# Seven block products per pair of column tiles: another order, and banks opened by ScalarE copies

## The chip, the cores and the metric

The kernel runs on one core of one Trainium2 chip. The metric is the device time of one execution in microseconds (us). The engines in this text: PE is TensorE (matmuls), PEld its loading of weights, DVE is VectorE, ACT is ScalarE, POOL is GpSimd, SP is SyncE, which here only issues DMAs.

## The reference, cut to what matters

One encoder block over 1024 positions and 1024 channels, batch 1, float32. The part that the change touches is the one big input projection of the normed input:

```python
hn = rms_norm(h, norm_in)
z = jnp.einsum('bsd,de->bse', hn, w_in)
zq, zkv, zkr, g_attn, u_pool, g_pool, g_merge = jnp.split(z, IN_SPLITS, axis=-1)
y_attn = mla_attention(zq, zkv, zkr, q_norm, w_uq, kv_norm, w_ukv) * jax.nn.silu(g_attn)
y_pool = multiscale_pool(u_pool, pool_w, pool_scale) * jax.nn.silu(g_pool)
a = jnp.einsum('bsc,cd->bsd', y_attn, w_branch_attn)
p = jnp.einsum('bsc,cd->bsd', y_pool, w_branch_pool)
gate_a, gate_p = jnp.split(jax.nn.sigmoid(g_merge.astype(jnp.float32)).astype(h.dtype), 2, axis=-1)
merged = gate_a * a + gate_p * p
h = h + jnp.einsum('bsd,de->bse', merged, w_out)
```

`g_attn`, `u_pool`, `g_pool` and `g_merge`, 3584 columns of `z`, are 28 tiles of 128 columns.

## The kernel before, in words

Every matrix product is made of three: each operand is split into a high part (rounded to the matmul's format) and a low rest, and high x high, high x low and low x high are added up. `split` (line 384) makes the two parts: a ScalarE copy (`acopy`, line 295) for the high part and a VectorE subtraction (`tt`, line 304) for the low one.

The stages: the latent projection of q (to about 40 us), the rotary key and the kv latent (to 72 us), then fourteen pairs (72 to 351 us), the up-projections (to 410 us), attention (to 566 us), the attention branch and its merge (to 616 us), and the output projection with the last norm.

A **pair** (class `Pair`, line 885) takes two of the 28 column tiles at once and all 1024 positions. Weights and input are cut into 2 x 2 blocks (two column tiles by two halves of the channels; two halves of the channels by two halves of the positions), and the four results c11, c12, c21, c22 (128 columns by 512 positions) are made with seven block products instead of eight. `ORDER` (line 889) names the weight block and the input block of each of the seven. S1 to S4 are sums and differences of weight blocks, made for each pair by VectorE (`both`, line 909); t1 to t4 are those of the input, made once (`block_sums`, line 575). `operand` (line 903) splits a weight block into a buffer of the kinds `wh` (2 buffers), `wl` (2) and `t` (45, shared by almost everything); which kind, goes by the operand's place in the order in which they are made.

A product (`product`, line 927) is 4 x 3 matmuls of 512 columns that add into one bank of PSUM. `run` (line 945) has three banks per pair: `b` is one of two buffers `p`; `a` and `c` are each one half of a two-bank tile (`ps`), and consecutive pairs take the left and the right half in turn. The sum in a bank is carried on by products that are added to what stands in it, and it is read out in between: by `acopy` or by `tt` into a result. `times` multiplies a result by the rows' 1/rms (`r`), and `posts` finish a result tile of both halves: a sigmoid or SiLU (ScalarE, the SiLU with two POOL multiplications) or the pooling windows, then a DMA that stores it.

`preps` (line 914) lists seven steps that make the operands of the *next* pair; `tick()` takes one after each product. Some pairs carry other work beside them (`beside`): `gate_pair(8, [(2, POOL_ITEMS[2]), (4, POOL_ITEMS[3])])` (line 1092) runs the third pool item's product ahead of the pair's product 2 and the fourth's ahead of product 4. A pool item loads its tile `d` two products earlier and splits it one product earlier.

None of this is the order on the engines. `Plan` (line 85) records all operations, and `order` (line 127) sets each engine's sequence by estimated costs: at each step it takes an operation that can start soonest, and among those within 30 ns of it the one written first. Each of the four `mms` groups of a product is one operation, so two products can be interleaved. Buffers of a kind are handed out in the order written. At run time every engine, and SP with its DMAs, works through its list in order and waits by semaphores.

Of the kernel before, what the change touches and what calls it, by code (L numbers as in the profile page):

```python
# [8 lines left out]
F32 = mybir.dt.float32  # L9
F32R = mybir.dt.float32r  # L10
AF = mybir.ActivationFunctionType
ALU = mybir.AluOpType
# [60 lines left out]
def real(x):  # L73
    return x.ap() if isinstance(x, View) else x
# [135 lines left out]
def hybrid_block_kernel(  # L210
# [30 lines left out]
    def buf(tag, cols, dt, name):  # L241
        uid[0] += 1
        nm = f"{name}_{uid[0]}"
        pool = pp if tag in PSUM else tp
        b = Buf(lambda: pool.tile([P, cols], dt, tag=tag, bufs=SLOTS[tag], name=nm), tag)
        b.nm = name
        return View(b, 0, P, 0, cols)
# [9 lines left out]
    def t32(name):  # L257
        return buf("t", T, F32, name)
# [5 lines left out]
    def psum(v):  # L264
        return isinstance(v, View) and v.buf.tag is not None and v.buf.tag in PSUM
# [29 lines left out]
    def acopy(o, x):  # L295
        plan.add(
            "ACT",
            lambda: nc.scalar.copy(real(o), real(x)),  # L298
            0.8333 * x.n + (155 if psum(x) else 190),
            [x],  # L300
            [o],
        )

    def tt(o, a, b, op, eng="DVE"):
        e = nc.vector if eng == "DVE" else nc.gpsimd
        c = 1.055 * a.n + 145 if eng == "DVE" else 2.2 * a.n + 150
        port = eng == "POOL" or not (psum(a) or psum(b))
        plan.add(eng, lambda: e.tensor_tensor(real(o), real(a), real(b), op), c, [a, b], [o], port=port)  # L308
# [162 lines left out]
    lft, rgt = slice(0, 512), slice(512, T)  # L471
# [4 lines left out]
    class Item:  # L476
        def __init__(self, src, width, kt, run):
            self.src, self.width, self.run, self.kt = src, width, run, kt
            self.tag = raw_tag[0]
# [75 lines left out]

    ORDER = [0, 4, 1, 5, 2, 6, 3, 7]
    raws = {k: start_loads(k) for k in ORDER[:3]}
    xs = [None] * 8
# [29 lines left out]

    for n, k in enumerate(ORDER):
        w, x = raws[k]  # L590
# [8 lines left out]
        for a in range(0, T, step_n):  # L599
            c = slice(a, a + step_n)  # L600
# [9 lines left out]
        if n + 3 < 8:  # L610
            raws[ORDER[n + 3]] = start_loads(ORDER[n + 3])
        h, l = xs[k]
# [19 lines left out]
    state = {}  # L632
# [252 lines left out]
    class Pair(Item):  # L885

        ORDER = (("A11", "b11"), ("S2", "t2"), ("S1", "t1"), ("S3", "t3"), ("A12", "b21"), ("A22", "t4"), ("S4", "b22"))

        def __init__(self, i, posts, beside=()):
            self.i, self.posts, self.beside = i, posts, dict(beside)
# [21 lines left out]
        def preps(self):  # L914
            self.ops = {}
            S, A = ALU.subtract, ALU.add
            return [
                lambda: (self.operand("A11"), self.operand("A22")),
                lambda: (self.both("S1", "A21", "A22", A, "A22"), self.both("S3", "A11", "A21", S, "A21")),
                lambda: (self.both("S2", "S1", "A11", S, "A11"), self.operand("S2")),  # L920
                lambda: self.operand("S1"),
                lambda: self.operand("S3"),
                lambda: self.operand("A12"),
                lambda: (self.both("S4", "A12", "S2", S, "A12"), self.operand("S4")),
            ]

        def product(self, bank, which, first):
# [4 lines left out]
            if which in self.beside:  # L932
                self.beside[which].go(self)
            a, b = self.ORDER[which]
            for k, ((ah, al), (bh, bl)) in enumerate(zip(self.ops[a], B[b])):
# [9 lines left out]
        def run(self, it, tick):  # L945
            if "acc" not in state:
                state["acc"] = [buf("s", T, F32, "ps") for _ in range(2)]
            half = (lft, rgt)[self.turn % 2]
            a, c = (v[:, half] for v in state["acc"])
            o1, o2 = t32("z"), t32("z")  # L950
            c11, c12, c21, c22 = o1[:, lft], o1[:, rgt], o2[:, lft], o2[:, rgt]

            def times(o, side):
                tt(o, o, state["r"][:, side], ALU.mult)

            self.product(a, 0, True)
            acopy(c21, a)
            tick()
            b = buf("p", 512, F32, "pb")
            self.product(b, 1, True)  # L960
            tt(c12, b, c21, ALU.add)
            tick()
            self.product(c, 2, True)
            tt(c22, c, c21, ALU.add)
            tick()
            self.product(b, 3, False)
            tt(c22, b, c22, ALU.add)
            times(c22, rgt)
            tick()
            self.product(a, 4, False)  # L970
            tt(c11, a, state["r"][:, lft], ALU.mult)
            tick()
            self.product(b, 5, False)
            tt(c21, b, c21, ALU.add)
            times(c21, lft)
            self.posts[1](o2)
            tick()
            self.product(c, 6, False)
            tt(c12, c, c12, ALU.add)
            times(c12, rgt)  # L980
            self.posts[0](o1)
            tick()

    loaded, ready = [0], [0]
# [203 lines left out]
    for h in range(HEADS):  # L1188
# [5 lines left out]
        for qr in range(4):  # L1194
            prs = []
            for i in (2 * qr, 2 * qr + 1):
# [17 lines left out]
                b, o = pr_of[i]  # L1214
# [33 lines left out]
            a = buf("oa", 256, F32, "oa")  # L1248
            r, c = (0, 64) if h % 2 == 0 else (64, 0)
# [14 lines left out]
    for i in range(8):  # L1264
# [9 lines left out]
        for n, (a, b) in enumerate(spans):  # L1274
            c = slice(a, b)
# [104 lines left out]
```

## Time and profile before

| what | value |
|---|---|
| median of 3 runs | 711.28 us (710.94, 711.28, 712.9) |
| the profiled execution's own time | 712.28 us |
| its span, first to last instruction | 710.2 us |
| busy: PE, DVE, ACT, POOL | 691.1 (97%), 524.2 (74%), 319.7 (45%), 104.8 us (15%) |
| matmuls | 3428 |
| granted TensorE clock, mean | 0.999 |

The time is that of the whole execution; the span leaves out what lies ahead of the first and behind the last instruction. A busy share is of the span. TensorE's matmuls are pipelined and their ends are modelled, so one is drawn longer than the distance to the next; distances from start to start are the safer measure. "[0.78 <-DVE z L308]" behind a row says that the engine was idle 0.78 us before it and that this idle time ended with VectorE's instruction of line 308 on a tile z. Line numbers are often those of a helper: 275 is every matmul, 298 every ScalarE copy, 308 every two-operand VectorE or POOL step, 377 every DMA.

### The profile page before, as it was taken

The numbers are of one execution on the slowest core, as the hardware profiler recorded it, in microseconds if no ns is written. First come the engines' busy times: TensorE is split into PE (matmuls) and PEld (weight loads), VectorE is DVE, ScalarE is ACT, GpSimd is POOL, SyncE is SP. The second block draws the span as 40 slices with busy tenths as digits, with TensorE's granted clock in tenths as the row PEclk, the third lists the DMA queues.
The fourth block names the chain that finished last, engine by engine and source line by source line (L and its number), as shares of the span: only waits on it lengthen the run. The fifth ranks groups of instructions, "written<-read, shape, count | busy, mean of one in ns | idle before, by whom it ended". The sixth has DMA issues, their size and how long they took to land.

```text
span 710.2 us, 9562 instructions
## 1 busy us (share of the span) xinstructions
PE 691.1 (97%) x3428; PEld 581.1 (82%) x3428; DVE 524.2 (74%) x823; ACT 319.7 (45%) x587; POOL 104.8 (15%) x140
## 2 busy tenths in 40 slices
PE   8999999999999999999998999999999999999996
PEld 6878888888878878888786799989999777888885
DVE  5688898777978689789869678887887859932223
ACT  5864424331423344333346467666666525421112
POOL 0020100300002030300101044545443100000000
PEclk9999999999999999999999999999999999999999
DMA  8957433122715436233777986554322499413131
GB/s 313 375 177 260 149 119 120 68 111 99 279 59 179 177 118 235 91 132 103 284 256 293 325 187 189 142 138 109 106 75 74 160 326 409 143 60 118 60 118 60
DMA packets 39567, 120.70 MB, mean 170 GB/s; under 512 B 5088, under 2 KB 6240, under 8 KB 39520
## 3 DMA queue, kind: packets, MB, share of 16 engines
q1 hardware_dynamic: 39520, 120.09, 49.4%
q8 instruction: 27, 0.44, 0.2%
q14 instruction: 20, 0.16, 0.1%
HBM read 81.14 MB, written 37.88 MB: 168 GB/s over the span
## 4 chain that ended last, share of the span: by engine, by line
PE 83%; DMA 6%; DVE 5%; ACT 2%; issue 2%; SPq 1%; DVEq 0%; ACTq 0%
PE ps L275 28%; PE pb L275 22%; PE po L275 12%; PE sc L275 7%; PE o L275 5%; PE pf L275 5%; PE pt L282 4%; DMA wr<-w_bp 2%; DMA wr<-w_uq 1%; DMA wo<-w_o 1%; DVE lo L308 1%; SPq L377 1%; DMA x<-xT 1%; DMA wr<-w_uv 1%; DVE ra L308 1%
## 5 line engine op out<-in xcount | busy, mean ns | idle before, releaser
L275 PE MATMUL pb<-t,wp 128*128 128x512 f32 x504 | 121.6, 390 | 0.0
L275 PE MATMUL ps<-xa,wp 128*128 128x512 f32 x392 | 113.0, 390 | 0.0
L275 PEld LDWEIGHTS pb<-t,wp 128*128 128x128 f32 x504 | 94.5, 188 | 19.8 <-DVE z L308 0.2
L298 ACT CAST wp<-wr 128x512 fp32r<-128x512 f32 x98 | 58.9, 619 | 102.2 <-DVE wr L308 38.3
L275 PEld LDWEIGHTS ps<-xa,wp 128*128 128x128 f32 x392 | 73.6, 188 | 15.2
L308 DVE TENSOR_TENSOR wp<-wr,wp 128x512 fp32r<-128x512 f32 x98 | 72.6, 756 | 8.8 <-ACT wp L298 8.8
L322 POOL TENSOR_SCALAR pr<-pr,small 128x384 f32<-128x384 f32 (+4 forms) x64 | 48.3, 759 | 72.1 <-DVE small L348 56.6
L290 ACT ACTIVATE pr<-sc,small 128x384 f32<-128x384 f32 (+4 forms) x64 | 47.7, 746 | 20.6 <-DVE small L357 19.7
L308 DVE TENSOR_TENSOR pT<-pt,pT 128x512 fp32r<-128x512 f32 (+1 forms) x80 | 48.6, 633 | 8.9 <-ACT pT L298 8.3
L357 DVE TENSOR_REDUCE small<-sc 128x1 f32<-128x128 f32 (+3 forms) x64 | 47.5, 750 | 9.2 <-PE sc L275 8.7
L308 POOL TENSOR_TENSOR z<-z,sig 128x512 f32<-128x512 f32 x16 | 23.5, 1493 | 199.7 <-ACT sig L290 197.3
L275 PE MATMUL po<-woh,hi 128*128 128x512 f32 (+1 forms) x136 | 51.3, 377 | 0.0
L275 PE MATMUL po<-woh,lo 128*128 128x512 f32 (+1 forms) x136 | 51.3, 377 | 0.0
L275 PE MATMUL po<-wol,hi 128*128 128x512 f32 (+1 forms) x136 | 51.2, 377 | 0.0
L298 ACT CAST pT<-pt 128x512 fp32r<-128x512 f32 (+1 forms) x80 | 41.2, 545 | 17.2 <-PE pt L282 16.5
L275 PE MATMUL o<-pT,v 128*128 128x256 f32 (+1 forms) x320 | 47.7, 282 | 0.6 <-DVE oa L308 0.4
L275 PEld LDWEIGHTS o<-pT,v 128*128 128x128 f32 x320 | 43.7, 189 | 3.2 <-DVE oa L308 0.8
L308 DVE TENSOR_TENSOR z<-pb,z 128x512 f32<-128x512 f32 x42 | 28.9, 689 | 23.3 <-PE pb L275 18.3
L308 DVE TENSOR_TENSOR res<-po,res 128x512 f32<-128x512 f32 (+1 forms) x17 | 11.2, 660 | 46.9 <-PE po L275 46.9
L275 PE MATMUL ps<-xb,wp 128*128 128x512 f32 x112 | 43.6, 389 | 0.0
L282 PE MATMUL pt<-ident,pr 128*128 128x128 f32 x288 | 42.1, 274 | 0.0
L275 PE MATMUL ps<-t,wp 128*128 128x512 f32 x168 | 41.1, 391 | 0.8 <-DVE z L308 0.8
(192 smaller groups left out, 1382.8 us busy)
## 6 DMA issues: line engine op xcount, KB each, us to landing
wr<-w_z SPq DMA_DIRECT2D x30, 512.0 KB, 4.9
gate_d<-z SPq DMA_DIRECT2D x16, 512.0 KB, 2.6
xt<-xr SPq DMA_DIRECT2D x8, 512.0 KB, 10.3
go<-gate_d SPq DMA_DIRECT2D x16, 256.0 KB, 2.8
mp_d<-go SPq DMA_DIRECT2D x16, 256.0 KB, 2.8
gate<-gate_d SPq DMA_DIRECT2D x8, 512.0 KB, 7.3
mp<-mp_d SPq DMA_DIRECT2D x8, 512.0 KB, 8.2
wo<-w_o SPq DMA_DIRECT2D x8, 512.0 KB, 8.7
```

What stands on the lines that cost most here:

```text
L275: nc.tensor.matmul(real(o), real(a), real(b), start=s, stop=e, **kw)
L282: nc.tensor.transpose(real(o), real(a), real(ident))
L290: nc.scalar.activation(real(o), real(x), func, scale=real(scale), **kw)
L298: lambda: nc.scalar.copy(real(o), real(x)),
L308: plan.add(eng, lambda: e.tensor_tensor(real(o), real(a), real(b), op), c, [a, b], [o], port=port)
L322: e.tensor_scalar(real(o), real(a), real(s1), real(s2), op0, op1)
L357: lambda: nc.vector.tensor_reduce(real(o), real(a), axis=AX.X, op=ALU.max, negate=True),
L377: lambda: nc.sync.dma_start(real(o), real(x)),
```

## The change

The seven products stay the same; their order, the bank of each, the order in which operands are made, and how results are read out are new. The first product (A11 x b11) now opens bank b, in which the running sums go on: b takes products 0, 2, 4 and 6, a takes 1, c takes 3 and 5. Results c11, c12 and c22 begin as ScalarE copies of a bank (three copies a pair, before it was one), and VectorE has seven steps on results (three additions, one multiplication out of a bank, three `times`), before it was nine.

```diff
--- before.py
+++ after.py
@@ -886,7 +886,7 @@
 
 
 
-        ORDER = (("A11", "b11"), ("S2", "t2"), ("S1", "t1"), ("S3", "t3"), ("A12", "b21"), ("A22", "t4"), ("S4", "b22"))
+        ORDER = (("A11", "b11"), ("A12", "b21"), ("S2", "t2"), ("S1", "t1"), ("S3", "t3"), ("S4", "b22"), ("A22", "t4"))
 
         def __init__(self, i, posts, beside=()):
             self.i, self.posts, self.beside = i, posts, dict(beside)
@@ -916,12 +916,12 @@
             S, A = ALU.subtract, ALU.add
             return [
                 lambda: (self.operand("A11"), self.operand("A22")),
-                lambda: (self.both("S1", "A21", "A22", A, "A22"), self.both("S3", "A11", "A21", S, "A21")),
-                lambda: (self.both("S2", "S1", "A11", S, "A11"), self.operand("S2")),
+                lambda: (self.operand("A12"), self.both("S1", "A21", "A22", A, "A22")),
+                lambda: (self.both("S3", "A11", "A21", S, "A21"), self.both("S2", "S1", "A11", S, "A11")),
+                lambda: self.operand("S2"),
                 lambda: self.operand("S1"),
-                lambda: self.operand("S3"),
-                lambda: self.operand("A12"),
-                lambda: (self.both("S4", "A12", "S2", S, "A12"), self.operand("S4")),
+                lambda: (self.operand("S3"), self.both("S4", "A12", "S2", S, "A12")),
+                lambda: self.operand("S4"),
             ]
 
         def product(self, bank, which, first):
@@ -953,32 +953,32 @@
             def times(o, side):
                 tt(o, o, state["r"][:, side], ALU.mult)
 
-            self.product(a, 0, True)
-            acopy(c21, a)
+            b = buf("p", 512, F32, "pb")
+            self.product(b, 0, True)
+            acopy(c11, b)
             tick()
-            b = buf("p", 512, F32, "pb")
-            self.product(b, 1, True)
-            tt(c12, b, c21, ALU.add)
+            self.product(a, 1, True)
+            tt(c11, a, c11, ALU.add)
+            times(c11, lft)
             tick()
-            self.product(c, 2, True)
-            tt(c22, c, c21, ALU.add)
+            self.product(b, 2, False)
+            acopy(c12, b)
             tick()
-            self.product(b, 3, False)
+            self.product(c, 3, True)
+            acopy(c22, c)
+            tick()
+            self.product(b, 4, False)
             tt(c22, b, c22, ALU.add)
             times(c22, rgt)
             tick()
-            self.product(a, 4, False)
-            tt(c11, a, state["r"][:, lft], ALU.mult)
-            tick()
-            self.product(b, 5, False)
-            tt(c21, b, c21, ALU.add)
-            times(c21, lft)
-            self.posts[1](o2)
-            tick()
-            self.product(c, 6, False)
+            self.product(c, 5, False)
             tt(c12, c, c12, ALU.add)
             times(c12, rgt)
             self.posts[0](o1)
+            tick()
+            self.product(b, 6, False)
+            tt(c21, b, state["r"][:, lft], ALU.mult)
+            self.posts[1](o2)
             tick()
 
     loaded, ready = [0], [0]
```

What becomes of it on the engines, from the two programs. On TensorE the number of instructions is the same. One place is where a pair ends and the next begins, the first pair with pool items beside it being the one that ends (the tile `ps_134` holds bank c of both pairs, one half each; `ps_133` holds bank a; `wp` are weight operands; xa and xb are parts of the input). Before:

```order
L275 MATMUL ps_134_746<-xa_53_263,wp_198_1491 128x512
L275 MATMUL ps_134_746<-xb_54_272,wp_198_1491 128x512
L275 MATMUL ps_134_746<-xa_53_263,wp_198_1491 128x512
L275 MATMUL ps_134_746<-t1_65_317,wp_220_1548 128x512 x3
L275 MATMUL ps_134_746<-t1_89_512,wp_220_1548 128x512 x3
L275 MATMUL ps_134_746<-t1_107_618,wp_220_1548 128x512 x3
L275 MATMUL ps_134_746<-t1_127_729,wp_220_1548 128x512 x3
L275 MATMUL pb_232_1636<-t2_66_344,wp_217_1618 128x512 x3
```

The first three rows are the end of the pair's S4 product into c; the next pair's S1 product follows at once into the other half of the same tile. After, at the same place of the program:

```order
L275 MATMUL ps_133_733<-xa_53_263,wp_213_1603 128x512
L275 MATMUL pb_230_1527<-t2_66_344,wp_220_1559 128x512 x3
L275 MATMUL pb_230_1527<-t2_90_515,wp_220_1559 128x512 x3
L275 MATMUL pb_230_1527<-t2_108_620,wp_220_1559 128x512 x3
L275 MATMUL pb_230_1527<-t2_128_737,wp_220_1559 128x512 x3
L275 MATMUL ps_134_769<-t1_65_317,wp_223_1570 128x512 x3
L275 MATMUL ps_134_769<-t1_89_512,wp_223_1570 128x512 x3
L275 MATMUL ps_134_769<-t1_107_618,wp_223_1570 128x512 x3
L275 MATMUL ps_134_769<-t1_127_730,wp_223_1570 128x512 x3
L275 MATMUL pb_230_1527<-t3_67_379,wp_224_1561 128x512 x3
```

Here the S1 product follows the S2 product (t2), which follows the A12 product into bank a (its last row stands first). The end of the earlier pair's S4 product stands 36 matmuls ahead of the first t1 row: t4 of that pair, then A12 and S2 of this one.

On SP, the DMAs around the loads of the third and fourth pool item (`d_d2`, `d_d3`; `ga_d` are stores of two SiLU results, `gp` and `y` belong to the pool items, `w_z` are weights). Before:

```order
L377 DMA d_270_2031<-d_d2_1485 128x1024
L377 DMA gp_271_2033<-gp_d2_1804 128x1024
L377 DMA ga_d1_2044<-z_255_1903 128x1024
L377 DMA d_277_2082<-d_d3_1435 128x1024
L377 DMA gp_278_2088<-gp_d3_1761 128x1024
L377 DMA ga_d0_2107<-z_254_1917 128x1024
L377 DMA y_d2_2120<-gp_271_2033 128x1024
```

After:

```order
L377 DMA d_271_2019<-d_d2_1435 128x1024
L377 DMA gp_272_2021<-gp_d2_1770 128x1024
L377 DMA ga_d0_2044<-z_254_1900 128x1024
L377 DMA ga_d1_2069<-z_255_1952 128x1024
L377 DMA d_278_2078<-d_d3_1479 128x1024
L377 DMA gp_279_2080<-gp_d3_1813 128x1024
L377 DMA y_d2_2118<-gp_272_2021 128x1024
```

Both SiLU stores now stand ahead of the load of the fourth pool item. The same place on ScalarE, after the change (`wp` are splits of weights, `hi` of the pool items, `z` the results):

```order
L298 CAST hi_275_2050<-d_271_2019 128x1024
L298 CAST wp_265_2056<-wr_240_1745 128x512
L298 COPY z_268_2036<-pb_270_1999 128x512
L298 CAST wp_273_2106<-wr_252_1837 128x512
L298 CAST hi_282_2112<-d_278_2078 128x1024
L298 COPY z_269_2126<-ps_134_769 128x512
L298 CAST wp_284_2131<-wr_252_1837 128x512
```

Two copies out of banks now stand among the casts, one of them directly behind the cast of the fourth pool item's tile; before there was none between the two `hi` casts or behind the second.

Where the last pair ends, SP before had the store of one gate result, the three loads of zq, the store of the other gate result and the load of `w_uq`; now it has the three loads of zq, the load of `w_uq`, and then both stores.

## Rows read from the trace of the kernel before

**Rows 1.** Busy time by stretch (x: instructions), the fourteen pairs and one full window.
```profile
72.00:353.00 281.00, 278.62 (x1239) 229.25 (x1239) 231.50 (x331) 99.92 (x150) 27.81 (x19) 1.00 0.41 147
92.00:111.00 19.00, 19.00 (x85) 15.73 (x84) 18.65 (x30) 5.92 (x9) 0.00 (x0) 1.00 0.30 112
```

**Rows 2.** Chain that ended last, 190 to 270 us: start us, us, what.
```profile
202.14 2.72 PE pb L275 x12
...
259.97 4.19 DMA d<-d_d
```

**Rows 3.** TensorE's waits, 72 to 360 us: us in total, times, longest us.
```profile
PE ps L275 <- DVE z L308: 0.8, 1, 0.8
PE pb L275 <- DVE zkv L308: 0.6, 1, 0.6
PE pb L275 <- DVE lo L308: 0.5, 1, 0.5
PE pb L275 <- ACT hi L298: 0.3, 1, 0.3
```

**Rows 4.** Timeline around 196 us: start, us, engine, instruction, [idle before <-releaser].
```profile
193.17 0.39 PE L275 MATMUL ps<-xa,wp 128*128 128x512 f32 x1
...
193.40 2.20 PE L275 MATMUL ps<-t,wp 128*128 128x512 f32 x9
...
195.64 0.69 DVE L308 TENSOR_TENSOR z<-ps,z 128x512 f32<-128x512 f32 x1 [0.69 <-PE ps L275]
...
196.38 0.97 PE L275 MATMUL ps<-t,wp 128*128 128x512 f32 x3 [0.78 <-DVE z L308]
```

**Rows 5.** Timeline, 249 to 267 us, the two pool items of one pair.
```profile
249.02 3.00 POOL L308 TENSOR_TENSOR z<-z,sig 128x512 f32<-128x512 f32 x2 [28.99 <-ACT sig L290]
...
259.78 0.61 PE L275 MATMUL pb<-hi,wh 128*128 128x512 f32 x2
259.97 0.32 SPq L377 DMA_DIRECT2D d<-d_d  x1
...
260.46 0.73 PE L275 MATMUL pb<-lo,wh 128*128 128x512 f32 x2
...
264.24 1.05 ACT L298 CAST hi<-d 128x1024 fp32r<-128x1024 f32 x1 [7.51 <-DMA d<-d_d]
...
264.68 0.39 PE L275 MATMUL ps<-xa,wp 128*128 128x512 f32 x1
...
265.34 0.73 PE L275 MATMUL pb<-hi,wh 128*128 128x512 f32 x2 [0.27 <-ACT hi L298]
...
266.60 0.73 PE L275 MATMUL pb<-lo,wh 128*128 128x512 f32 x2 [0.53 <-DVE lo L308]
```

**Rows 6.** Timeline of TensorE, of VectorE and of ScalarE, 344 to 353 us.
```profile
350.15 0.39 PE L275 MATMUL ps<-xa,wp 128*128 128x512 f32 x1
351.15 1.07 PE L275 MATMUL pb<-hi,wh 128*128 128x512 f32 x2 [0.61 <-DVE zkv L308]
352.05 0.62 PE L275 MATMUL pb<-lo,wh 128*128 128x512 f32 x2
...
346.78 1.23 DVE L308 TENSOR_TENSOR lo<-zq,hi 128x1024 fp32r<-128x1024 f32 x1 [1.22 <-ACT hi L298]
...
349.12 2.47 DVE L308 TENSOR_TENSOR zkv<-zkv,pb 128x512 f32<-128x512 f32 x4
...
344.96 0.84 ACT L298 CAST wh<-wr 128x768 fp32r<-128x768 f32 x1 [2.56 <-DMA wr<-w_uq]
```

**Rows 7.** Groups, 72 to 353 us: xcount | busy us, mean ns | idle before <-releasers.
```profile
L308 DVE TENSOR_TENSOR z<-pb,z 128x512 f32<-128x512 f32 x42 | 28.9, 689 | 23.3 <-PE pb L275 18.3 <-ACT wp L298 2.1 <-ACT z L298 1.5
...
L298 ACT COPY z<-ps 128x512 f32<-128x512 f32 x14 | 8.1, 577 | 2.6 <-PE pb L275 1.6 <-PE ps L275 1.0
```

**Rows 8.** TensorE's waits, 360 to 412 us.
```profile
PE ps L275 <- DVE wl L308: 1.5, 1, 1.5
PE pv L275 <- DVE ul L308: 1.3, 1, 1.3
```

## The prediction

> **What bounds the kernel now.** I read the stretch of the fourteen pairs, 72 to 353 us, since the change touches nothing outside it. First the table by stretches: of 281.00 us there TensorE is busy 278.62, VectorE 231.50, ScalarE 99.92, at a granted clock of 1.00, which is the upper of TensorE's two levels [rows 1]. A matmul's end is modelled, so I check this against the chain that ended last: twelve matmuls of 512 columns follow each other in 2.72 us, 0.227 us each, although each is drawn longer [rows 2]. 14 pairs x 7 products x 12 matmuls x 0.227 us make 267 us, and the change alters none of them. What it can alter is only the time in which TensorE stands still. The list of TensorE's waits has four entries in the stretch, 2.2 us in all [rows 3]. Measured from start to start they are longer, because the modelled end of the last matmul hides the first part of each stop. There are three places:
>
> - 196 us [rows 4]: nine matmuls start at 193.40 and take 9 x 0.227 = 2.04, so the next was due at 195.44; it starts at 196.38: **0.94 us**.
> - 260 to 267 us, the two pool items [rows 5]: due 259.78 + 0.45 = 260.23, start 260.46: **0.23**. Then due 264.68 + 0.23 = 264.91, start 265.34: **0.43**. Then due 265.34 + 0.45 = 265.79, start 266.60: **0.81**.
> - 351 us, the last pair running into the q products [rows 6]: due 350.15 + 0.23 = 350.38, start 351.15: **0.77**; the two matmuls from there were due to end at 351.60 and the next starts at 352.05: **0.45**.
>
> Together 3.63 us, 0.5% of the run. That is the ceiling of what the change can give inside its stretch, whatever it takes off VectorE.
>
> **The change part by part.**
>
> *Two VectorE steps fewer, two ScalarE copies more, per pair.* The trace groups VectorE's result steps: z<-pb,z 42 times at 689 ns [rows 7], three a pair. The new order needs one of those a pair, so 28 x 0.689 = 19.3 us leave VectorE; 28 copies at 577 ns [rows 7] = 16.2 us come to ScalarE. VectorE falls from 231.5 to about 212 us in the stretch, ScalarE rises to about 116 of 281. Neither is on the path: between 92 and 111 us VectorE is busy 18.65 of 19.00 us and TensorE still 19.00 of 19.00 [rows 1]. So this is worth nothing by itself; it is worth something only where a stop above ends on a VectorE step that comes earlier.
>
> The Trainium skill (Perfetto Trace Analysis, section Optimizing Scalar/DVE Operations) says that work may be moved to ScalarE when VectorE is saturated. By that rule the 19.3 us would come off the end; by the rows only a part of 3.63 us can.
>
> *The reopened banks.* Bank b is now written by products 0, 2, 4 and 6 and read out after each, bank c by 3 and 5. Before a bank is written again, its reader must be done. The product between covers that: 2.72 us [rows 2] against a copy of 0.58 [rows 7]. Cost nothing, as long as the copy starts within about 2.1 us of its product's end. If the cover is gone (the copy stands behind other ScalarE work), TensorE waits for the rest; the longest common ScalarE instruction here is 1.05 [rows 5], and one of them fits. I allow 0.2 us in all for single reopenings that lose the race, between 0 and 28 x 0.1 = 2.8 if every copy lost by a tenth.
>
> *The stop at 196.* VectorE's step z<-ps at 195.64 had been idle 0.69 us for TensorE [rows 4], although its own product ended with the matmul of 193.17. It waited for the nine matmuls of the next pair's S1 product. These write the other half of the same tile (the pairs alternate halves of one tile for bank c), and both orders are kept by tile: the step waits for nine matmuls that do not concern it, and the last three matmuls wait for the step. Before, c's last product (place 6) and the next pair's first one in c (place 2) lie 3 products apart; now they are places 5 and 3, 5 apart, and the order on TensorE shows at this place the products with t4, b21 and t2 between them, 36 x 0.227 = 8.2 us, against a step of 0.69. This stop goes: **-0.94**.
>
> *The stops at 260 to 267.* The last two end on the load of d for the fourth pool item: SP issues it at 259.97, it lands 4.19 us later [rows 2], ScalarE's cast has waited 7.51 us for it, and VectorE's split comes after the cast [rows 5]. SP issued it at 259.97 because its buffer, one of the t slots, came free with the A12 product: its last matmul is the one ahead of the pool item's first at 259.78, so it starts at 259.55 and, drawn 0.39 us long as all of 512 columns are [rows 4], ends at 259.94; SP begins at 259.97 [rows 5]. In the new order A12's operand lies in a wl slot and the t slots hold A22, S2 and S3; the load takes the slot that S2 leaves, two products earlier. From the end of t2 to the fourth pool item TensorE has 9 + 6 + 3 + 12 + 9 = 39 matmuls, 8.84 us. Needed are 4.19 + 1.05 (cast) + 1.23 (split, of the same 1024 columns as the zq split in [rows 6]) = 6.5 us. So 0.43 + 0.81 go: **-1.24**. The 0.23 before them ends on VectorE's split of the third item, whose load had long landed; it stands behind other VectorE work, before and after. I take nothing for it, with 0 to 0.23 as the ends.
>
> *The stop at 351.* TensorE waits for VectorE's four zkv products, which free the bank. They stand behind a split of zq that waited 1.22 us for ScalarE's cast, which in turn stood behind a cast that waited 2.56 us for the load of w_uq [rows 6]. The new order puts that load on SP ahead of both gate stores instead of between them, which brings it earlier by one 512 KB transfer; but it also puts a bank copy between the casts. The ends are nothing and all of 1.22; I take the middle: **-0.61**.
>
> *What lies behind.* The next stops, 1.5 and 1.3 us for VectorE's wl and ul between 360 and 412 us [rows 8], belong to the up-projections and are the same instructions in the same order. I move nothing there.
>
> Sum: -0.94 - 1.24 - 0.61 + 0.2 = -2.6 us. The profiled execution took 712.28 us, 2.1 more than its span; 712.28 - 2.6 = 709.7. It is 1.0 above the median of the three runs (711.28), so against the median I forecast **708.7 us**.
>
> **The rivals.**
>
> *B, only the stop at 196 goes.* The other two hang on loads, and a load that is asked for earlier can still land late: SP works in order, and the store ahead of d on SP now waits for POOL's two multiplications, 3.00 us [rows 5]. For it: two of three stops name a DMA behind the engine. Against it: the margin of 8.84 over 6.5 us. Time: 711.28 - 0.94 = 710.3, no change that can be told.
>
> *C, a copy behind a cast that waits for a load (slower).* On ScalarE the new order puts the copy of bank c directly behind the cast of d for the fourth pool item. ScalarE runs in order; if the load is late, the copy is late, and TensorE's S4 product into c waits. From t2's end to that reopening are 30 matmuls, 6.80 us; the load, the cast and the copy need 4.19 + 1.05 + 0.58 = 5.8, so it decides from a load that lands about 1 us later than the one before. As a price I take the wait that the same cast had, 7.51 us [rows 5]: 7.51 + 1.05 + 0.58 - 2.72 = 6.4 us of stop, with the 1.24 not gained: 711.28 + 6.4 - 0.94 - 0.61 = 716.1. For it: the two rows stand next to each other in the order. Against it: the load is issued earlier by two products.
>
> The Trainium skill (Perfetto Trace Analysis, section Matmuls) wants independent groups of matmuls rotated through different banks, so that reading one out overlaps the next. It speaks against the change, since four of the seven products now share bank b; the rows say that one product of another bank in between is cover enough.
>
> *D, the margin carries on.* VectorE has less to do at the end of the stretch, and the stops of 1.5 and 1.3 us [rows 8] go too, with all of the 3.63: 711.28 - 6.4 = 704.9. For it: both end on VectorE. Against it: VectorE is not behind there, it waits for casts and loads.
>
> *E, VectorE sets the pace after all:* 711.28 - 19.3 = 692.0, against the row of 92 to 111 us.
>
> **How the numbers follow.** I give the forecast 0.55, B 0.32, D 0.07, C 0.05, E 0.01. A measurement of this kernel can tell about 0.3%, 2.1 us, from no change. The forecast, D and E are faster by more: 0.63; B is within: 0.32; C is slower: 0.05. The range: the forecast's own ends are 711.28 - 3.63 = 707.65 (all three stops gone, nothing new) and 711.28 - 2.18 + 0.2 = 709.3 (nothing of the stop at 351); B reaches to 711.3 with a reopening loss of 1 us. Runs of one kernel lay 2 us apart, so I take 0.9 off the lower end. From 706.8 to 711.4 the forecast and nearly all of B are in; D, C and E are left out.
>
> **What would show it.** Right: in the stretch of the pairs the list of TensorE's waits has no VectorE z entry, the entry for the cast of d is gone, and SP issues the last load of d some 8 us ahead of its first matmul; VectorE's result steps are 98 instead of 126, ScalarE's copies 42 at about 0.58 us; TensorE's 0.227 us per matmul is unchanged. Wrong: a wait of TensorE for ScalarE's copy z in a pair (the cover was too thin), a wait for d as long as before (B or C), or a stop at the start of the q products that is as long as the one of 351 us.

## The result, and the profile after

The kernel with the change takes 708.96 us in the median (20 runs, 705.72 to 713.33); the kernel before, run beside it, 712.55 (20 runs). The ratio is 0.9949, with a 95% interval of 0.9931 to 0.9968: 3.6 us faster, between 2.3 and 4.9. The prediction was 708.7 us, a gain of 2.6. On a second chip the same kernel stood at 0.9934 (0.9910 to 0.9959).

The profiled execution has a span of 706.7 us, 3.5 less than before. First the table by stretches, for the fourteen pairs, as in [rows 1]:

```profile
72.00:353.00 281.00, 280.98 (x1255) 232.73 (x1254) 216.83 (x308) 117.31 (x180) 28.68 (x19) 1.00 0.42 148
```

TensorE is busy all but 0.02 of 281 us, VectorE 216.83 instead of 231.50, ScalarE 117.31 instead of 99.92. (VectorE's busy time fell by 14.7 and not by the 19.3 us forecast. Part of this is the fixed window: the change does all its 98 result steps in it and already two more splits of what follows, the kernel before only 123 of its 126.) The list of TensorE's waits from 68 to 360 us, which had four entries [rows 3], is empty. The groups show the exchange of steps, in the columns of [rows 7]:

```profile
L308 DVE TENSOR_TENSOR z<-pb,z 128x512 f32<-128x512 f32 x14 | 9.6, 688 | 3.1 <-ACT wp L298 2.1 <-PE pb L275 0.8 <-ACT z L298 0.2
...
L298 ACT COPY z<-pb 128x512 f32<-128x512 f32 x28 | 16.3, 583 | 28.6 <-PE pb L275 28.6
```

The z<-pb,z steps fell from 42 to 14, and 28 copies of bank b are new, 583 ns each, as forecast from 577. Now the three places. The one of [rows 4], in the timeline (start us, us, engine, instruction, idle before it):

```profile
192.29 0.69 DVE L308 TENSOR_TENSOR z<-ps,z 128x512 f32<-128x512 f32 x1
...
196.26 2.88 PE L275 MATMUL pb<-t,wp 128*128 128x512 f32 x12
...
198.98 2.88 PE L275 MATMUL ps<-t,wp 128*128 128x512 f32 x12
```

The last step that reads the earlier pair's half of c ends at 192.98; the next pair writes c from 198.98, at once after the twelve matmuls that began at 196.26 (12 x 0.227 = 2.72). Before, the reading step stood between the ninth and the tenth matmul into the other half.

The pool items, against [rows 5]:

```profile
256.30 0.32 SPq L377 DMA_DIRECT2D d<-d_d  x1
...
261.25 1.05 ACT L298 CAST hi<-d 128x1024 fp32r<-128x1024 f32 x1
...
258.14 0.61 PE L275 MATMUL pb<-hi,wh 128*128 128x512 f32 x2
258.78 0.74 PE L275 MATMUL pb<-lo,wh 128*128 128x512 f32 x2
259.36 0.63 PE L275 MATMUL pb<-hi,wl 128*128 128x512 f32 x2
...
265.30 0.62 PE L275 MATMUL pb<-hi,wh 128*128 128x512 f32 x2
265.76 0.61 PE L275 MATMUL pb<-lo,wh 128*128 128x512 f32 x2
```

The last load of d goes out 9.0 us ahead of its first matmul (265.30), where the forecast said some 8; the cast at 261.25 has no idle time in front of it, where it had 7.51, and the fourth item's matmuls follow one another without a stop. What remains is the stop of the third item: 258.14 + 0.45 = 258.59, start 258.78, so 0.19.

The end of the last pair, against [rows 6]:

```profile
332.45 0.33 SPq L377 DMA_DIRECT2D wr<-w_uq  x1
332.83 2.12 SPq L377 DMA_DIRECT2D gate_d<-z  x2
...
339.21 0.84 ACT L298 CAST wh<-wr 128x768 fp32r<-128x768 f32 x1 [0.85 <-PE ps L275]
...
344.64 2.47 DVE L308 TENSOR_TENSOR zkv<-zkv,pb 128x512 f32<-128x512 f32 x4
...
345.32 2.88 PE L275 MATMUL pb<-t,wp 128*128 128x512 f32 x12
348.04 0.62 PE L275 MATMUL pb<-hi,wh 128*128 128x512 f32 x2
```

The load of w_uq stands ahead of both gate stores, ScalarE's cast no longer waits for it (2.56 us before), VectorE's zkv products end at 347.1, and the q products start where they were due: 345.32 + 2.72 = 348.04. The whole stop is gone.

To compare kernels I add up TensorE's stops from start to start: the distance between the starts of two matmuls beyond what the columns of the first take (0.227 us for 512), wherever it is over 0.06 us. From 72 to 360 us that was 4.23 us before and is 0.59 after. The difference, 3.64, is the 3.5 us of the span. From 360 us on the stops are the same (15.7 us before and after).

### The profile page after: what moved, and what is told of

It reads as the page before. It is cut to its first block, busy times and chain, and to the rows that moved or that the text cites. A ratio compares the mean times of both kernels' runs of the same rounds, so it can differ in the third digit from the quotient of the medians.

```text
span 706.7 us, 9554 instructions
## 1 busy us (share of the span) xinstructions
PE 689.4 (98%) x3428; PEld 581.5 (82%) x3428; DVE 505.4 (72%) x795; ACT 334.5 (47%) x615; POOL 105.6 (15%) x140
## 4 chain that ended last, share of the span: by engine, by line
PE 91%; DVE 3%; DMA 2%; ACT 1%; issue 1%; SPq 0%; DVEq 0%; ACTq 0%
PE pb L275 29%; PE ps L275 26%; PE po L275 12%; PE sc L275 7%; PE pf L275 5%; PE o L275 5%; PE pt L282 4%; PE pv L275 1%; DMA wr<-w_bp 1%; DMA x<-xT 1%; DVE lo L308 1%; DVE ra L308 1%; DMA wr<-w_uv 1%; ACT hi L298 0%; DVE rb L366 0%
## 5 line engine op out<-in xcount | busy, mean ns | idle before, releaser
L275 PE MATMUL ps<-xa,wp 128*128 128x512 f32 x224 | 73.9, 390 | 0.0
L275 PEld LDWEIGHTS ps<-xa,wp 128*128 128x128 f32 x224 | 42.0, 188 | 8.7
L290 ACT ACTIVATE junk<-res 128x512 f32<-128x512 f32 (+1 forms) x17 | 10.3, 607 | 66.5 <-DVE res L308 66.5
```

Source lines behind the costliest of these rows:

```text
L275: nc.tensor.matmul(real(o), real(a), real(b), start=s, stop=e, **kw)
L290: nc.scalar.activation(real(o), real(x), func, scale=real(scale), **kw)
```

## Experiments

All times are ratios to the kernel before on the same chip. "Stops" is the sum just described in the profiled execution of each kernel, 72 to 360 us.

| kernel | median us | before | ratio, 95% interval | stops |
|---|---|---|---|---|
| before | | | 1 | 4.23 |
| the change | 708.96 | 712.55 | 0.9949, 0.9931 to 0.9968 | 0.59 |
| the change, second chip | 708.10 | 711.93 | 0.9934, 0.9910 to 0.9959 | 0.58 |
| change, copies on VectorE | 709.63 | 711.26 | 0.9970, 0.9946 to 0.9994 | 3.55 |
| before, two steps fewer | 711.13 | 711.26 | 0.9988, 0.9966 to 1.0010 | 1.65 |
| before, three steps fewer | 709.14 | 711.93 | 0.9955, 0.9935 to 0.9975 | 2.36 |
| before, d loaded earlier | 709.66 | 711.26 | 0.9966, 0.9944 to 0.9988 | 3.59 |
| before, a and c in one tile | 717.06 | 711.26 | 1.0070, 1.0046 to 1.0095 | 8.73 |
| change, a and c in one tile | 710.11 | 712.32 | 0.9968, 0.9950 to 0.9985 | 3.02 |
| change, two steps put back | 710.48 | 712.32 | 0.9975, 0.9954 to 0.9996 | 3.39 |
| change, each copy four times | 714.37 | 712.32 | 1.0038, 1.0018 to 1.0058 | 7.64 |
| before, second raw slot | 710.24 | 711.93 | 0.9967, 0.9944 to 0.9991 | 2.11 |
| change, second raw slot | 706.86 | 712.32 | 0.9926, 0.9905 to 0.9948 | 0.30 |
| the same, y splits moved | 706.93 | 711.93 | 0.9908, 0.9877 to 0.9939 | 0.30 |

Taking steps away, adding them, or changing slots also lets the planner place other instructions elsewhere; where that matters it is said.

**The copies on VectorE: order and banks alone.**

```diff
-            acopy(c11, b)
+            vcopy(c11, b)
```

and the same for c12 and c22.

> The changed kernel with its three bank copies a pair made by VectorE instead of ScalarE: the new order and banks, but ten result steps on VectorE, one more than the kernel before had. Theory (the 3.5 us came off because the new order moved two waits and a load; how many steps VectorE has is beside the point): nearly all of the gain stays, 2 to 3.5 us under the kernel before; the stops at 196, 265 to 267 and 351 us stay away, and at most one or two new stops under 1 us appear. Rival (the gain is VectorE's relief): VectorE has 1 step a pair more than before instead of 2 fewer, so the gain goes and the time is that of the kernel before or above it (14 x 0.58 = 8 us more on VectorE at most).

The stops at 196, 265 to 267 and 351 us are away although VectorE has ten steps a pair, one more than before. But three new ones are there, the largest longer than any that went, and the stop of the third pool item (0.34 us before, with the slower start behind it) is 0.74. Rows of that kernel's timeline:

```profile
341.95 1.03 PE L282 MATMUL pb<-ident,small 128*128 128x128 f32 x8
344.40 0.47 PE L275 MATMUL ps<-xa,wp 128*128 128x512 f32 x1 [1.42 <-DVE z L352]
...
340.00 3.65 DVE L308 TENSOR_TENSOR lo<-zq,hi 128x1024 fp32r<-128x1024 f32 x3
343.57 0.68 DVE L352 COPY z<-ps 128x512 f32<-128x512 f32 x1
```

The copy that frees bank c stands on VectorE behind 3.65 us of zq splits, and TensorE waits for it (1.58 us from start to start); two more of 0.53 and 0.28 are at 100 and 177 us, where b is reopened. The stretch gains 0.68 us instead of 3.64. So the new order removes these stops without any relief of VectorE, and ScalarE's copies are what keeps new ones from taking their place. By the stops, the theory's "nearly all of the gain stays" fell. The time can't tell: 2.1 us faster (0.4 to 3.8) is within the 2 to 3.5 of the theory, and this execution's stops up to 45 us were 1.0 us shorter than those of the kernel before. The rival's "no gain" fell: the old stops are gone without it.

**Two steps fewer in the old order**, the rival by itself.

```diff
             tt(c22, b, c22, ALU.add)
-            times(c22, rgt)
...
             tt(c21, b, c21, ALU.add)
-            times(c21, lft)
```

> The kernel before, in its old order with its old banks, without two of its nine VectorE steps a pair: two of the four results of a pair are not multiplied by 1/rms. VectorE has 28 x 0.69 = 19 us less to do, as in the change. Theory: nothing, within 0.7 us of the kernel before; the stops at 196 (0.94 us), 265 to 267 (1.24) and 351 us (1.22) stand where they stood, save that the one at 351 us, behind a queue on VectorE, may shrink by up to half. Rival (VectorE's relief): 3.5 us faster, as the change was. Second rival (VectorE sets the pace): 19 us faster.

The stop at 196 us stands as before (0.95, then 0.11). The ones at 265 to 267 and 351 us are gone, with only 0.32 left at 270. That is against the theory, which gave nothing. But it is not relief alone, for the planner also moved the pool items and the loads:

```profile
258.91 0.32 SPq L377 DMA_DIRECT2D d<-d_d  x1
...
268.24 0.62 PE L275 MATMUL pb<-hi,wh 128*128 128x512 f32 x2
```

The last load of d goes out 9.3 us ahead of its first matmul here, about as in the change (9.0); in the kernel before it was 5.4 (259.97 and 265.34). The load of w_uq follows both gate stores and lands 6.6 us after its issue instead of 8.1; ScalarE's cast waits 0.35 us for it instead of 2.56. The time did not show the gain: 0.9 us faster, with an interval from 2.4 faster to 0.7 slower. In this execution TensorE's stop at 378 us is 2.43 instead of 1.61 and its first 12 us ran longer at the lower clock (last section).

**Three steps fewer**, the same with a larger dose (the step on c12 left out as well).

> The kernel before, in its old order with its old banks, without any of the three multiplications by 1/rms that stand as steps of their own: three of the four results of a pair are not multiplied by it, and VectorE has six steps a pair, 42 x 0.69 = 29 us less. Theory (two of the three stops end on VectorE being behind, the one at 196 us on the order of the banks): the stop at 196 us stands at 0.9 us, the ones at 265 to 267 and at 351 us are gone or under 0.3 us, so 2 us under the kernel before, between 1 and 2.6. Rival (relief on VectorE is worth nothing in the old order): within 0.7 us of the kernel before. Second rival (VectorE sets the pace): 29 us faster.

TensorE's list of waits from 68 to 360 us:

```profile
PE ps L275 <- DVE z L308: 0.8, 1, 0.8
PE pb L275 <- DVE lo L308: 0.2, 1, 0.2
```

The first is the stop at 196 us, with 29 us of VectorE work taken away; 351 is gone, 265 to 267 too, and what is left there is 0.78 around 258 us, at the third item. It is 3.2 us faster (1.8 to 4.6); in its profiled execution the stops are 1.9 us shorter in the stretch and 1.1 us behind it, up to 412 us. Here too the loads moved with the order: the last load of d goes out 6.8 us ahead of its matmul (258.11 and 264.91), and w_uq lands after 6.2 us. So the stop at 196 does not yield to relief; whether the other two would yield to relief in an unchanged order, these two kernels do not show.

**The load of d one product earlier, in the old order.**

```diff
-            if which + 2 in self.beside:
-                self.beside[which + 2].load()
+            for k in self.beside:
+                if which == (1 if (self.i, k) == (22, 4) else k - 2):
+                    self.beside[k].load()
```

> The kernel before with one edit: the load of the fourth pool item is asked for one product earlier. Theory: the two stops of TensorE at 265.3 and 266.6 us (0.43 + 0.81) go and the rest stays, so 1.2 us under the kernel before; the ends are 0.4 and 1.5. Rival (the load is issued when its slot comes free and not when it is asked for, or it is slowed by what else is moving then): the wait of ScalarE's cast for the load stays at 5 us or more and the time does not change.

```profile
253.20 0.32 SPq L377 DMA_DIRECT2D d<-d_d  x1
...
256.66 2.01 ACT L298 CAST hi<-d 128x1024 fp32r<-128x1024 f32 x2 [1.48 <-PE ps L275]
```

SP issues the load at 253.20 (259.97 before), both casts of d run together and wait for TensorE, not for a DMA, and the stops from 230 to 275 us fall from 1.69 to 0.19, by more than the 1.24 that I had counted. A stop of 0.85 at 182 us, which the kernel before doesn't have and only the one with the second raw slot shows too (0.79), hides part of it in the sum; the time is 2.4 us lower (0.9 to 4.0). The load is a cause of that stop.

**The banks of one pair in one tile.** Two kernels test whether waits are kept by the tile.

```diff
-            half = (lft, rgt)[self.turn % 2]
-            a, c = (v[:, half] for v in state["acc"])
+            tile_ = state["acc"][self.turn % 2]
+            a, c = tile_[:, lft], tile_[:, rgt]
```

> The kernel before with banks a and c of one pair as the two halves of one tile and the next pair in the other tile, instead of halves that alternate: the same banks, matmuls and steps. Theory (waits are kept by the tile, so a step that reads one half waits for matmuls that write the other): the stop at 196 us goes, but inside every pair steps on a and matmuls into c now wait for one another: new stops of 0.5 to 1.5 us at four to eight pairs, 3 to 7 us slower than the kernel before. Rival (waits are kept by the half): no step waits for a matmul of the other half, and the time is within 0.7 us of the kernel before.

Slower by 5.0 us (3.3 to 6.8), with the stop at 196 away. One of the new stops, in its timeline:

```profile
110.04 0.39 PE L275 MATMUL ps<-xa,wp 128*128 128x512 f32 x1
111.21 0.50 PE L275 MATMUL ps<-xa,wp 128*128 128x512 f32 x1 [0.78 <-DVE z L308]
...
110.47 0.69 DVE L308 TENSOR_TENSOR z<-ps,rstd 128x512 f32<-128x512 f32 x1 [1.50 <-PE ps L275]
```

VectorE's step on a sits idle 1.50 us until the matmul of 110.04, which writes c, is done; then TensorE's next matmul into c waits for that step, although it writes the other half. It is the pattern of [rows 4], now inside a pair, with the same 0.94 us from start to start.

The same edit on the change:

> The changed kernel with banks a and c of one pair as the two halves of one tile, pairs alternating between the two tiles. Theory (waits are kept by the tile): in the new order a is written by product 1 and read out while c is written by product 3, with b between, so that a step on a must be late by a product to cost anything; where VectorE is behind, TensorE stops: two to four stops of about 0.7 to 1.1 us, so 2 to 4 us slower than the change, about the time of the kernel before. Rival (waits are kept by the half): the change's own time, 3.5 us under the kernel before.

TensorE's list of waits has VectorE's z twice, 0.8 each (101.7 and 179.7 us, 0.95 from start to start), and of the change's gain in the stretch 1.2 us is left. The time, 2.3 us under the kernel before (1.1 to 3.6), lies between the two forecasts; the list of waits decides. Two kernels, same banks, same matmuls, only other tiles: the tile is the unit in which readers and writers wait for one another here. This is a matter of how the program's semaphores are set; `Plan` itself compares column ranges (`_hit`), so its order does not foresee these waits.

**Two steps put back on VectorE.**

```diff
             tt(c22, b, c22, ALU.add)
+            tt(c22, c22, c22, ALU.max)
             times(c22, rgt)
```

and the same for c12.

> The changed kernel with two more VectorE steps of 128x512 in each pair (the larger of a result and itself, which changes nothing in it): new order, new banks, ScalarE's copies, but VectorE has nine steps a pair as before. First theory (the order alone made the gain): still 2.5 to 3.5 us under the kernel before, and TensorE's list of waits in the stretch of the pairs stays empty. Second theory, formed after the first four runs (the new order gains only as long as VectorE has room at two or three tight places: beside the zkv and pool items): one to three stops of 0.5 to 2.3 us come back, and the time is 0 to 2.5 us under the kernel before.

By its numbers the second theory holds: 1.8 us under the kernel before (0.3 to 3.3), one large stop (2.44 us at 188) and one of 0.45 at 354. Only the small one is VectorE's: a step that reads a bank comes late, and TensorE waits for it. None of the old stops is back. The large one is worth reading. First this kernel (the first line is from SP's list of waits), then the change at the same place:

```profile
SPq L377 <- DVE wl L308: 4.3, 1, 4.3
...
180.10 0.33 SPq L377 DMA_DIRECT2D wr<-w_uq  x1
180.48 0.42 SPq L377 DMA_DIRECT2D d<-d_d  x1
...
185.84 1.04 ACT L298 CAST hi<-d 128x1024 fp32r<-128x1024 f32 x1 [4.08 <-DMA d<-d_d]
186.80 0.61 ACT L298 CAST wp<-wr 128x512 fp32r<-128x512 f32 x1
187.31 0.58 ACT L298 COPY z<-ps 128x512 f32<-128x512 f32 x1
...
187.95 0.50 PE L275 MATMUL ps<-xa,wp 128*128 128x512 f32 x1 [2.27 <-ACT z L298]
```

```profile
176.56 0.42 SPq L377 DMA_DIRECT2D d<-d_d  x1
...
182.98 0.33 SPq L377 DMA_DIRECT2D wr<-w_uq  x1
...
184.15 1.06 ACT L298 CAST hi<-d 128x1024 fp32r<-128x1024 f32 x1 [2.55 <-DMA d<-d_d]
185.11 0.57 ACT L298 COPY z<-ps 128x512 f32<-128x512 f32 x1
...
186.74 0.39 PE L275 MATMUL ps<-xa,wp 128*128 128x512 f32 x1
```

That is rival C: ScalarE's copy of bank c stands behind a cast that waits for the load of d, and TensorE waits for the copy. Here the load went out 3.9 us later, and not because VectorE was behind: the planner put the load of w_uq ahead of it on SP (in the change it stands behind), and SP waited 4.3 us for the split `wl` that frees the one raw slot. That split ended at 180.07, earlier than in the change (182.95). So this run shows 0.45 us as the price of the added steps, and leaves the rest open. In the change itself the copy ends at 185.68 and the bank is wanted at 186.74, so that it passes with 1.06 us to spare.

**Each copy four times**, the cover.

```diff
-            acopy(c11, b)
+            for _ in range(4):
+                acopy(c11, b)
```

> The changed kernel with each of its three bank copies a pair made four times: 4 x 0.58 = 2.3 us of ScalarE where 0.58 stood, against a cover of 2.72 us by the product between (and 42 x 3 x 0.58 = 73 us more on ScalarE, 190 of 281 us in the stretch). Theory (the cover is one product less one copy, 2.1 us): the cover is nearly used up, so TensorE stops for ScalarE at reopenings of b where a cast or a sigmoid of 1.05 us stands ahead of a copy, some ten stops of 0.2 to 2.2 us, 7 to 12 us slower than the change. Rival (there is more cover than that, since the copies are read out behind products of other banks): under 2 us slower. Rival (a bank is held to the end of the whole pair): as fast as the change.

```profile
203.12 2.44 ACT L298 COPY z<-pb 128x512 f32<-128x512 f32 x4 [2.04 <-PE pb L275]
...
202.92 2.20 PE L275 MATMUL ps<-t,wp 128*128 128x512 f32 x9
205.61 1.66 PE L275 MATMUL pb<-t,wp 128*128 128x512 f32 x6 [0.49 <-ACT z L298]
```

Stops of 0.65 at 205.6, 225.5 and 245.3 us, where the planner has left only nine matmuls (9 x 0.227 = 2.04 us) between two products into b; where there are twelve, even 2.44 us of copies are covered. The rest is at the pool items and at 350 us (1.73). 6.3 us slower than the change by the two ratios, a little under the 7 to 12 forecast. One copy of 0.58 is nowhere near the limit unless something waits in front of it.

**A second raw slot in the old order**, for the load of w_uq.

```diff
-SLOTS = {"t": 45, "wr": 1, "wh": 2, "wl": 2, "go": 2, "oa": 2, "s": 2, "p": 2, "o": 1, "f": 1}
+SLOTS = {"t": 44, "wr": 2, "wh": 2, "wl": 2, "go": 2, "oa": 2, "s": 2, "p": 2, "o": 1, "f": 1}
```

> The kernel before with a second slot for raw weights (wr), paid for with one of the 45 slots of t: the load of w_uq can be issued before the slot of the last pair is free. Theory (the stop of 1.2 us at 351 us begins with that load, which ScalarE's cast awaited for 2.56 us): the cast no longer waits for it and the stop at 351 is gone or under 0.4; the stop of 1.6 us at 376 us, where TensorE waits for the split of w_uk, goes too; those at 196 and 265 us stay: 1.5 to 2.8 us under the kernel before. Rival (VectorE is behind there with or without that load): the stop at 351 stays at 0.8 us or more.

```profile
343.00 0.84 ACT L298 CAST wh<-wr 128x768 fp32r<-128x768 f32 x1 [0.60 <-PE pb L275]
```

The load for this cast went out at 186.79 us already. The cast does not wait for a DMA, the stop at 351 us is gone, and so is the one at 376; those from 360 to 412 us fall from 5.71 to 3.82 in all. The stop at 196 stays. (Those at 265 to 267 went too, which was not expected: with one t slot fewer the last load of d goes out 6.6 us ahead of its matmul.) As with d, the load is a cause.

**Faster versions.** The second slot on the change:

> The changed kernel with two slots for raw weights of the projections (wr) instead of one, paid for with one of the 45 slots of t. An attempt at a faster version: the stop of 1.6 us at 375 us, where TensorE waits for the split of w_uk, should go, since that load needs no longer wait for the slot. Theory (each stop is let go by its own load): the stop at 375 goes and the one at 386 us stays or grows by up to 1 us: 0.5 to 1.6 us under the change. Rival (VectorE is the bound between 360 and 390 us): what goes at 375 comes back at 386, and the time is the change's.

and with three of the four splits of y moved behind the k projections:

```diff
-            if which == "k":
+            if which == "k" and p in (0,):
                 yp[p] = split_tile(yp[p])
...
             wh, wl = shared["v"]
+            for y in {1: (1,), 3: (2,), 5: (3,)}.get(j, ()):
+                yp[y] = split_tile(yp[y])
```

> The changed kernel with the second raw slot of the run before it, and with three of the four splits of y, 1.22 us each, moved from the k projections (VectorE busy without a pause from 367 to 386 us) to the v projections behind them. An attempt at a faster version. Theory (each further stop has a cause of its own that can be moved): the stops at 375 and 384 us both go and at most one of 0.9 us appears behind them: 2 to 3 us under the change. Rival (VectorE is as full behind 386 us): the stop reappears at 390 to 402 us and the time is that of the second raw slot alone, about 2 us under the change.

Beside the last one ran the change once more:

> The change itself, to stand beside the next kernel on the same chip: 3.6 us under the kernel before (2.3 to 4.9 by the interval of its first measurement).

Both versions beat the kernel before, by 5.3 and 6.5 us. In the first the stop at 375 is gone, the one at 386 stays (1.67 us at 383.7), and by the ratios it is 1.6 us under the change, the upper end of its theory. The second is 1.2 us lower than the change beside it (706.93 and 708.10). The intervals of both overlap with that of the change: probably faster, not shown. TensorE's waits from 360 to 620 us say where part of it went, first of the change beside it, then of the version with the splits moved:

```profile
PE pv L275 <- DVE ul L308: 1.6, 1, 1.6
PE ps L275 <- DVE wl L308: 1.4, 1, 1.4
```

```profile
PE ps L275 <- DVE wl L308: 1.7, 1, 1.7
PE sc L275 <- DMA kl<-kn_d: 1.1, 1, 1.1
```

The two stops aimed at (375 and 386 us) are gone; the 1.7 is another, at 590 us, which every execution has in some size (0.3 to 1.9), and the wait for the reload of the keys, 1.1 us at 411, is in both versions and not in the change: TensorE now gets there before the stored k projections are back.

## Why the prediction was right

The bound was read rightly: no more could come off than TensorE's stops in the stretch, 3.64 us did, and 19.3 us of steps on VectorE were not worth 19.3. That the forecast time lies 0.3 us from the measured one is luck: the 711.28 us that it starts from, the median of three runs, was 1.3 below the median of twenty, and the gain was forecast 1.0 too small. Point by point:

- *The stop at 196, -0.94.* Right in size (1.05 went, with the slower start behind the stop), and the cause is shown: it stood in all four old-order kernels in which neither banks nor tiles were changed, also with 29 us less on VectorE, and sharing a tile made the same stop in other places.
- *The stops at 260 to 267, -1.24.* Right; 1.38 went. The load went out 9.0 us ahead of its matmul, and an earlier load alone does it too. In the kernels of this text in which these two stops are gone, the load leads its matmul by 6.6 us or more, against the 6.5 that I had added up and the 5.4 of the kernel before.
- *The stop at 351, -0.61.* **This is the term that was mis-sized: all 1.22 went, and I took half.** I had argued that the load of w_uq comes earlier "by one 512 KB transfer" and that a copy between the casts could eat it. The load was issued 4.37 us earlier (332.45 for 336.82), of which 2.4 are the stops that were gone by then, and in its new place, ahead of the stores and 4.8 us behind the loads of zq, it took 3.5 us to land instead of 8.1. No copy stood between that cast and the zq casts behind it, and ScalarE had 0.85 us idle in front of it.
- *Lost reopenings, +0.2.* None: the list has no wait for a copy. They come only when a copy's engine is late, as on VectorE or with four copies.
- *"Worth nothing by itself."* Not refuted, and not tested alone. 19 us less in the old order left 1.65 us of stops out of 4.23, but with the loads of d and w_uq in other places. The other way round, the stops at 265 and 351 stayed away with VectorE at ten steps a pair (copies on VectorE) and at nine (two steps put back). So the order with its loads is enough for these two. What room on VectorE is worth is seen elsewhere: it keeps new stops of 0.28 to 1.58 us from arising when banks are read out.

The 0.61 too little and the 0.2 that didn't come are 0.81 of the 0.9 us between forecast (2.6) and span (3.5). Rival B held one stop; three went. D (the stops behind 360 us go too) didn't happen. C has not happened, and the runs show its mechanism one load away. Of the two rules of the Trainium skill: Perfetto Trace Analysis, section Optimizing Scalar/DVE Operations, says only that moving work to ScalarE may make sense when VectorE is saturated; that 19.3 us would come off was my own reading of it, and the measured gain is 3.6. Section Matmuls of that page of the Trainium skill, on rotating banks, is not contradicted: with four copies, or with one that came late, a reopened bank did stop TensorE, by 0.65 to 2.4 us at a time, and with one copy of 0.58 under 2.04 us of cover it cost nothing.

What stays open: whether less work on VectorE would end the stops at 265 and 351 in an unchanged order, since every kernel with fewer steps also had its loads moved; which part of the faster landing of w_uq is due to its place ahead of the stores; and why two steps fewer gained less in time (0.9 us) than in stops (2.6), with an interval that reaches 2.4.

## What to carry to other kernels

When one engine is busy 97% of the span, list its stops from start to start and follow each to its last cause: that sum, not the work moved, is what a change can give. Two halves of one tile are one thing to whoever waits for it; put what different steps read and write in different tiles, or far apart in the order. If a bank is reopened after one product of another bank, put its read-out on the engine with room and look at what stands in front of it: a load awaited by a cast holds the bank as a long copy would. When a trial takes steps away or adds some, see where the loads and products went before the steps get the credit.

## What the runs showed of the hardware

**A stop costs more than its length.** After most stops the second matmul starts about 0.34 us after the first, not 0.227 (196.38 and 196.72 before); in the rows of the change above, 258.78 to 259.36 is 0.58 for two matmuls of 0.45. I had left most of these 0.11 us out.

**The clock at the start differs between executions of one kernel.** From 8 to 10 us, first the change, then the same kernel on the second chip (the columns are those of [rows 1]; the one ahead of the last two is the granted clock):

```profile
8.00:10.00 2.00, 1.99 (x9) 1.65 (x10) 1.04 (x2) 1.48 (x2) 0.00 (x0) 1.00 1.02 384
```

```profile
8.00:10.00 2.00, 2.00 (x5) 1.57 (x6) 1.05 (x2) 1.55 (x2) 0.00 (x0) 0.56 1.04 395
```

Nine matmuls against five: in the second the granted clock is 0.56, near the lower of the two levels (1.2 of 2.4 GHz), and the stops up to 45 us add up to 5.7 us instead of 4.2. Ahead of the stretch TensorE had been idle for ScalarE in both, 1.56 us in the first and 1.21 in the second. Over all runs they lay between 2.6 and 6.4, which is as much as the change is worth: only medians, or the stops of one stretch, compare these kernels.

**VectorE beside GpSimd.** In the change, around 131 us:

```profile
131.05 5.95 POOL L308 TENSOR_TENSOR z<-z,sig 128x512 f32<-128x512 f32 x4 [54.69 <-ACT sig L290]
...
131.18 0.69 DVE L308 TENSOR_TENSOR z<-pb,rstd 128x512 f32<-128x512 f32 x1 [0.70 <-PE pb L275]
131.79 1.10 DVE L308 TENSOR_TENSOR wp<-wr,wp 128x512 fp32r<-128x512 f32 x1
...
134.60 2.95 DVE L308 TENSOR_TENSOR wp<-wr,wp 128x512 fp32r<-128x512 f32 x2 [1.71 <-ACT wp L298]
```

Beside GpSimd's multiplications a VectorE step with an operand in a bank takes its usual 0.69 us, and one with both operands in SBUF 1.10 to 1.5 instead of 0.69. No stop came of it here: TensorE's list of waits in the stretch is empty.
